# A hybrid attention and state-space layer: input squares, norms and decay sums placed by hand, and the output projection's first tiles loaded ahead

## The chip, the cores and the metric

The kernel runs on one NeuronCore of one Trainium2 chip. The metric is device time in microseconds (us) of a whole execution. Five engines run side by side: TensorE (PE, matmuls and transposes; PEld is its weight load), VectorE (DVE), ScalarE (ACT), GpSimd (POOL) and SyncE (SP), which here issues the DMAs. Each engine works through its own instruction list, so an instruction that waits holds back all that stands behind it there.

## The reference

The layer works on 2048 tokens of width 1024. The input is normalized, projected by one wide matrix `w_in`, and split among three groups of heads whose gated results are joined to 2048 columns, projected by `w_out`, added to the input and normalized again:

```python
hn = rms_norm(h, norm_in_w)
q, k, v, g_attn, z, xbc, dt_raw, q_mem, g_mem = split(hn @ w_in)
att = window_attention(rotary(q), rotary(k), v, sink) * silu(g_attn)      # 16 heads, 4 key heads, +-128 tokens
xs, bm, cm = split(silu(centred_depthwise_conv(xbc)))                     # 5 taps
y = ssd_scan(xs, dt[0], ...) + reversed(ssd_scan(reversed ...)) + d_skip * xs   # state-space scan, both directions
ssd = gated_group_rmsnorm(y, z, ssd_norm_w)
xat = softmax(q_mem @ mk.T) @ mv * silu(g_mem)                            # 4 heads onto 256 memory tokens
h = h + concat([att, ssd, xat]) @ w_out
return rms_norm(h, norm_out_w)
```

Inside a 128-token block the scan needs exp of differences of cumulative sums (the decay sums); from block to block a state is carried, once backward and once forward.

## The kernel before

**Tiling.** All is float32. Each product is three PE matmuls on high and low halves (`split3` L183); the halves come from an ACT cast to the high part (L195) and a DVE subtraction of the low one (L196). Nearly all PE matmuls carry the line of the helper `mm`, L177, so rows are told apart by their tiles. Weights of 128x1024 are loaded into `ws` (two buffers), or `xr` in the output projection, and split into `wh`, `wl` (three buffers each).

**Stages.** The main program walks four chunks of 512 tokens, from the last to the first (`for c` L920). A chunk computes keys, values and time steps, then four groups g of heads, each followed by two convolution pieces, the gate z and the memory heads' projections. After the chunks comes the output projection over sixteen blocks of 128 tokens (L957 on): `load_w` fetches the first weight tiles, `load_wo` the others, `early(c)` (L1004) does the attention and memory part of a block whose scan part is not ready, `out_block(c)` a whole block. `mixed` loads a block's joined results from DRAM (`mix_d`) into `mxl` and casts them to `mxh`.

**Side tasks.** Attention, memory attention, the scan's local part (`ssd_local`: load `xc` and the decay rows `fb`, decay sums L610 and L611, their exp L612, then the products), the carried states (`incoming`) and the joined forward result (`forward`) are generators. PE's order is written out by a planner: `mm` and `tr` advance a planner clock, and between two pieces of main work `tick` lets the side tasks take a step. `yield x` says that the task's next step is not due before x us of planner time; `limits` say how many tasks of a kind run at once, `need` runs tasks until one is done, `idle` lets planner time pass. ACT, DVE, POOL and SP are ordered by a list scheduler from priorities and readiness; it may place an instruction ahead of others that were written before it.

**Around the change.** The norm of the chunk after the present one is made in pieces: `rstd_cols` (called by `cols_x` at g = 1) loads 128x512 halves of x into `cu`, three buffers shared with the convolution, and takes squares with a row sum on ACT (L302), 28 in all; `norm_x` at the end of g = 2 loads the transposed input into `xp` and scales it on DVE (L349), 24 in all, storing it to `xn_d`. In `ssd_local` the next part's loads and decay sums are taken one step ahead of its products. In `forward`, y (L782) and z (L784) are loaded into `b0` and `b1`, POOL adds the carried part (L787) and multiplies by z (L789), ACT squares (L790), DVE adds the pairs (L792), and PE sums them.

Of the kernel before, what the change touches and what calls it, by code (L numbers as in the profile page):

```python
# [10 lines left out]
F32 = mybir.dt.float32  # L11
F32R = mybir.dt.float32r
# [24 lines left out]
def as32(ap):  # L37
    return ap.bitcast(F32)
# [7 lines left out]
def layer(ctx: ExitStack, tc: tile.TileContext, a: dict):  # L46
# [66 lines left out]
    clock = [0.0]  # L113
    queues = {"att": [], "mem": [], "ssd": [], "inc": [], "fwd": []}
    limits = {"att": 3, "mem": 1, "ssd": 1, "inc": 1, "fwd": 1}
    active = {k: [] for k in queues}
# [62 lines left out]
    def tr(out, in_):  # L179
        clock[0] += 0.11  # L180
        nc.tensor.transpose(out, in_, ident)  # L181

    def split3(out, pairs, start=True, stop=True):  # L183
# [109 lines left out]

    def rstd_cols(src, nblk):

        ss = misc.tile([P, 8], F32, name="ss", bufs=2)
        s2 = misc.tile([P, 2, 8], F32, name="s2")
        for b in range(nblk):
            for j in range(2):
# [6 lines left out]
        return ss  # L306

# [20 lines left out]
    def cols_x(c):  # L328
        s, _ = window(c)
        w = CH * (c + 1) - s  # L330
        return rstd_cols(a["x"][s:s + w, :], w // P)
# [10 lines left out]
    def norm_x(c, rb):  # L342
# [257 lines left out]
    def ssd_load(c, g):  # L600
        dt, fc, win = dts[c]
        xc = sp.tile([P, 4, P], F32, name="xc", bufs=2)
        nc.sync.dma_start(xc, xbc_d[4 * g:4 * g + 4, :, c * P:(c + 1) * P].rearrange("j p t -> p j t"))
        fb = sp.tile([P, 2, 4, P], F32, name="fb", bufs=1)
        nc.sync.dma_start(fb, f_d[c * 16:(c + 1) * 16].rearrange("(d h) t -> d h t", d=2)[:, 4 * g:4 * g + 4, :]
                          .partition_broadcast(P))
        ee = sp.tile([P, 4, P], F32, name="b0")
        for r in range(4):
            hd = slice(4 * g + r, 4 * g + r + 1)
            nc.scalar.activation(ee[:, r], fb[:, 0, r], AF.Identity, bias=fc[:, 0, hd])  # L610
            nc.vector.scalar_tensor_tensor(ee[:, r], fb[:, 1, r], fc[:, 1, hd], ee[:, r], ALU.add, ALU.min)  # L611
        nc.scalar.activation(ee, ee, AF.Exp)  # L612
        return xc, ee

    def ssd_local(blocks):
# [78 lines left out]
    def mem_attention(c, hd, qh, ql, gm, mkt, mvt):  # L694
# [48 lines left out]
    def incoming(c):  # L743
# [30 lines left out]
    def forward(c):  # L774

        if c == 0:
            while not ssd_t.done:
                yield 1.0
# [141 lines left out]
    for c in range(NPER - 1, -1, -1):  # L920
# [4 lines left out]
        for g in range(NG):  # L925
            if c and g == 1:
                cols = cols_x(c - 1)
            if c and g == 2:
                dg = diag_x(c - 1, cols)
            if g >= 2:  # L930
# [7 lines left out]
            if c and g == 2:  # L938
                norm_x(c - 1, rows_x(c - 1, dg))
            for i in range(2 * g, 2 * g + 2) if c else ((0, 1, 2, 3, 4), (5, 6, 7), (), ())[g]:  # L940
# [9 lines left out]
        if c == 0:  # L950
            fwd = [spawn("fwd", forward(b)) for b in range(NB)]
        if c:
            with tc.high_priority(offset=200):
                xs = prep_x(c - 1)
# [4 lines left out]
    for k in WO_K[:3]:  # L959
        woh[k], wol[k] = load_w(a["w_out"][k * P:(k + 1) * P, :])  # L960
    wx.close()
# [21 lines left out]
    def mixed(c, qs):  # L983

        mh, ml = {}, {}
        for q in qs:
            lo = fp.tile([P, 4, P], F32R, name="mxl", bufs=6)
            nc.sync.dma_start(as32(lo), mix_d[4 * q:4 * q + 4, :, c * P:(c + 1) * P].rearrange("j p t -> p j t"))  # L988
            hi = fp.tile([P, 4, P], F32R, name="mxh", bufs=5)
            split(hi, lo, as32(lo))  # L990
            for j in range(4):
                mh[4 * q + j], ml[4 * q + j] = hi[:, j], lo[:, j]
        return mh, ml

# [67 lines left out]
    rest_wo()  # L1062
    while last > 3 and not fwd[1].done:
        main(early(last))
        last -= 1
# [72 lines left out]
```

## Time and profile before

| what | value |
|---|---|
| time, median of three runs | 1852.75 us (1848.21 to 1855.27) |
| the profiled execution, its own time | 1848.8 us |
| its span, first to last instruction | 1847.1 us |
| mean granted TensorE clock | 0.985 of full |
| PE busy | 1755.7 us, 95% |
| DVE, ACT, POOL busy | 64%, 50%, 14% |
| DMA | 61% of sixteen engines, 188 GB/s |

PE is busy in 95% of the span, so its idle stretches are the first thing to look for, and behind each of them the instruction that ended it. A row of a timeline gives start and duration in us, engine, source line, operation, the tiles written and read, and in brackets the idle time before it with what ended that. The granted clock is the share of full speed, 0.5 or 1 at any moment.

### The profile page before, as it was taken

Reading aid. Unit: us, or ns where it says so; the run is one execution under the profiler, and the core shown is the slowest. Engines: PE = TensorE matmul, PEld = TensorE weight load, DVE = VectorE, ACT = ScalarE, POOL = GpSimd, SP = SyncE. Lnnn points to the kernel's source line nnn. Section 1 sums busy time; section 2 is a strip of 40 time slices with the busy share of each in tenths; the row PEclk is TensorE's granted clock in tenths of the full one; section 3 lists DMA queues with packets and bytes.
Section 4 is the critical chain, followed back from the end, with each engine's and each line's share of the span. In section 5 each row is a group of like instructions: output and inputs, shape, how many; then the busy total and the mean of one; then the engine's idle time right before and its main releaser. Section 6 shows DMA issues by size and latency. Waiting matters only on the chain. (4 is left out here: it accounts for less than half of the span.)

```text
span 1847.1 us, 26627 instructions
## 1 busy us (share of the span) xinstructions
PE 1755.7 (95%) x9242; PEld 1426.0 (77%) x9242; DVE 1179.9 (64%) x2681; ACT 921.4 (50%) x1985; POOL 260.3 (14%) x253
## 2 busy tenths in 40 slices
PE   7889999999799999999999989999998999999998
PEld 6878878877578787777778877778776777787886
DVE  7466666688576667778666777977677543443443
ACT  6237645664665566657555654656566411111121
POOL 1000000012200000121000002210111133333321
PEclk9989999999899999999999989999998999999999
DMA  7666364578653854776475466673658586566553
GB/s 237 211 197 187 123 214 146 152 241 244 210 169 122 268 165 150 240 245 206 142 211 161 133 205 195 190 214 118 197 179 265 165 251 182 164 180 180 171 176 120
DMA packets 264422, 347.59 MB, mean 188 GB/s; under 512 B 29536, under 2 KB 172000, under 8 KB 264288
## 3 DMA queue, kind: packets, MB, share of 16 engines
q1 hardware_dynamic: 264288, 345.90, 61.1%
q8 instruction: 73, 1.20, 0.3%
q14 instruction: 61, 0.50, 0.1%
HBM read 254.34 MB, written 91.49 MB: 187 GB/s over the span
## 5 line engine op out<-in xcount | busy, mean ns | idle before, releaser
L177 PE MATMUL pj<-xh,wh 128*128 128x512 f32 (+2 forms) x1296 | 506.6, 391 | 2.8 <-ACT xh L195 1.0
L177 PE MATMUL pj<-xl,wh 128*128 128x512 f32 (+2 forms) x1296 | 494.0, 381 | 4.8 <-DVE xl L196 4.8
L177 PE MATMUL pj<-xh,wl 128*128 128x512 f32 (+2 forms) x1296 | 494.7, 382 | 0.9 <-DVE wl L196 0.8
L196 DVE TENSOR_TENSOR wl<-ws,wh 128x1024 fp32r<-128x1024 f32 (+2 forms) x175 | 212.3, 1214 | 117.3 <-ACT wh L195 112.9
L177 PEld LDWEIGHTS pj<-xh,wl 128*128 128x128 f32 x1296 | 246.0, 190 | 46.9 <-DVE wl L196 2.7
L177 PEld LDWEIGHTS pj<-xh,wh 128*128 128x128 f32 x1296 | 246.7, 190 | 41.9 <-issue 3.7
L177 PEld LDWEIGHTS pj<-xl,wh 128*128 128x128 f32 x1296 | 246.8, 190 | 40.7 <-DVE xl L196 5.9
L195 ACT CAST wh<-ws 128x1024 fp32r<-128x1024 f32 (+2 forms) x175 | 180.0, 1029 | 179.3 <-PE pj L177 127.6
L546 DVE CUSTOM_DVE_ANT_0 pm<-s,band,sink 128x384 f32<-128x384 f32 (+1 forms) x256 | 150.3, 595 | 48.3 <-PE s L177 46.4
L554 ACT ACTIVATE pm<-pm,mx 128x385 f32<-128x385 f32 (+1 forms) x256 | 151.2, 595 | 55.5 <-DVE mx L552 55.5
L177 PE MATMUL pj<-woh,mxh 128*128 128x512 f32 x416 | 169.1, 407 | 0.0
L177 PE MATMUL pj<-woh,mxl 128*128 128x512 f32 x416 | 164.2, 395 | 0.0
L177 PE MATMUL pj<-wol,mxh 128*128 128x512 f32 x416 | 164.1, 394 | 0.0
L648 POOL TENSOR_TENSOR b<-nat,win 128x256 f32<-128x256 f32 x64 | 43.3, 697 | 841.2 <-ACT nat L632 841.2
L558 ACT ACTIVATE pm<-pm,den 128x384 f32<-128x384 f32 (+1 forms) x256 | 133.5, 595 | 6.9 <-DVE den L556 6.8
L572 ACT COPY pt<-t 128x512 f32<-128x512 f32 x120 | 69.4, 583 | 103.6 <-PE t L181 103.3
L195 ACT CAST mxh<-mxl 128x512 fp32r<-128x512 f32 x64 | 39.5, 617 | 162.8 <-DMA mxl<-mix_d 105.7
L181 PE MATMUL t<-ident,pm 128*128 128x128 f32 x736 | 103.8, 276 | 11.6 <-ACT nat L632 6.7
L181 PEld LDWEIGHTS t<-ident,pm 128*128 128x128 f32 x736 | 86.5, 142 | 34.6 <-ACT nat L632 7.6
L177 PE MATMUL s<-khh,qs 128*128 128x384 f32 (+1 forms) x256 | 94.7, 370 | 18.3 <-DVE mx L546 13.8
L484 DVE SCALAR_TENSOR_TENSOR cu<-raw,cw,cu 128x512 f32<-128x512 f32 (+2 forms) x128 | 99.3, 776 | 3.3 <-ACT cu L482 2.0
L177 PE MATMUL o<-pt,vg 128*64 128x256 f32 x736 | 93.8, 388 | 1.6 <-DVE dq L425 0.7
(222 smaller groups left out, 2842.8 us busy)
## 6 DMA issues: line engine op xcount, KB each, us to landing
ws<-in_w_in_dram SPq DMA_DIRECT2D x152, 512.0 KB, 4.2
q_d<-rt SPq DMA_DIRECT2D x32, 512.0 KB, 4.3
qs<-q_d SPq DMA_DIRECT2D x32, 512.0 KB, 6.1
fb<-f_d SPq DMA_DIRECT2D x32, 512.0 KB, 4.4
mxl<-mix_d SPq DMA_DIRECT2D x64, 256.0 KB, 4.1
mix_d<-ao SPq DMA_DIRECT2D x64, 128.0 KB, 3.5
xc<-xbc_d SPq DMA_DIRECT2D x32, 256.0 KB, 3.7
st_d<-carry SPq DMA_DIRECT2D x32, 256.0 KB, 3.9
```

The lines of the kernel that those rows point to most:

```text
L177: nc.tensor.matmul(out, lhsT=lhsT, rhs=rhs, start=start, stop=stop)
L181: nc.tensor.transpose(out, in_, ident)
L195: nc.scalar.copy(hi, x)
L196: (eng or nc.vector).tensor_tensor(lo, x, as32(hi), ALU.subtract)
L484: nc.vector.scalar_tensor_tensor(u, raw[:, r0 + k:r0 + k + cnt], cw[:, i, k:k + 1], u, ALU.mult, ALU.add)
L546: nc.vector.tensor_tensor_reduce(pm[:, r, :w], ss[:, :w], band[:, ms], 1.0, sink8[:, 4 * g + r:4 * g + r + 1], ALU.add, ALU.max, mx[:, r:r ...
L554: nc.scalar.activation(pm[:, r, :w + 1], pm[:, r, :w + 1], AF.Exp, bias=mx[:, r:r + 1], scale=0.125, accum_out=den[:, r:r + 1])
L558: nc.scalar.activation(pm[:, r, :w], pm[:, r, :w], AF.Copy, scale=den[:, r:r + 1])
L572: nc.scalar.copy(pts[j], tt)
L648: nc.gpsimd.tensor_tensor(xd[:, d], nat[:, 0:256].rearrange("p (r e) -> p r e", r=4), win[:, d, 4 * g:4 * g + 4].unsqueeze(2).broadcast_to ...
```

## The change

The squares and the scaling of the next chunk become side tasks of a new kind, "io", that load several tiles ahead and do one instruction per step; each such instruction is held by `pin` behind the instruction of its engine that was written just before it. The squares' task starts at g = 0 and uses `xp` (four buffers) in place of `cu`; the scaling task starts at g = 2. The decay sums move to the start of their own part, with the first of four head rows pinned. `forward` may run two blocks at once, with y in a buffer of its own kind. The output projection's first two joined tiles are loaded into the `ws` buffers before the `w_in` weights' pool is closed, and its later odd weight tiles no longer use `ws`.

```diff
-    limits = {"att": 3, "mem": 1, "ssd": 1, "inc": 1, "fwd": 1}
+    limits = {"att": 3, "mem": 1, "ssd": 1, "inc": 1, "fwd": 2, "io": 1}
+    pin = tc.keep_in_program_order
...
-    def rstd_cols(src, nblk):
+    def cols_x(c, out):
...
-                xn = misc.tile([P, XW], F32, name="cu", bufs=3)[:, :CH]
-                nc.sync.dma_start(xn, src[b * P:(b + 1) * P, j * CH:(j + 1) * CH])
-                nc.scalar.activation(xn, xn, AF.Square, accum_out=s2[:, j, b:b + 1])
+        for _ in range(3):
+            load()
+        yield 8.0
+        for i, (b, j) in enumerate(jobs):
+            pin(nc.scalar.activation(tiles[i], tiles[i], AF.Square, accum_out=s2[:, j, b:b + 1]))
+            load()
+            yield 3.0
...
         for kt in range(KT):
-            x32 = misc.tile([P, XW], F32, name="xp", bufs=4)[:, :w]
-            nc.sync.dma_start(x32, a["xT"][kt * P:(kt + 1) * P, s:s + w])
-            nc.vector.scalar_tensor_tensor(x32, x32, nw[:, kt:kt + 1], rb[:, :w], ALU.mult, ALU.mult)
-            nc.sync.dma_start(xn_d[kt, :, s:s + w], x32)
+            if kt == 4:
+                yield 6.0
+            pin(nc.vector.scalar_tensor_tensor(tiles[kt], tiles[kt], nw[:, kt:kt + 1], out["rows"][:, :w],
+                                               ALU.mult, ALU.mult))
+            nc.sync.dma_start(xn_d[kt, :, s:s + w], tiles[kt])
+            load()
+            yield 2.0
...
+    def ssd_decay(c, g, fb):
...
+            i1 = nc.scalar.activation(ee[:, r], fb[:, 0, r], AF.Identity, bias=fc[:, 0, hd])
+            i2 = nc.vector.scalar_tensor_tensor(ee[:, r], fb[:, 1, r], fc[:, 1, hd], ee[:, r], ALU.add, ALU.min)
+            if r == 0:
+                pin(i1)
+                pin(i2)
...
-            xc, ee = nxt
+            xc, fb = nxt
+            ee = ssd_decay(c, g, fb)
...
-        yield 3.0
+        yield 4.5
...
-        yield 7.0
+        yield 8.5
...
-        yy = sp.tile([P, 4, P], F32, name="b0")
+        yy = sp.tile([P, 4, P], F32, name="xc", bufs=2)
-        zz = sp.tile([P, 4, P], F32, name="b1")
+        zz = sp.tile([P, 4, P], F32, name=f"b{c % 2}")
...
-        yield 11.0
+        yield 13.0
...
+    first = [wsp.tile([P, D], F32R, name="ws", bufs=2).rearrange("p (u j t) -> p u j t", u=2, j=4) for _ in range(2)]
+    first = mixed_tiles(NB - 1, (0, 3), *([t[:, 0], t[:, 1]] for t in first))
     wx.close()
...
+    idle(clock[0] + 3.0)
...
-        ws = wsp.tile([P, D], F32, name="ws", bufs=2) if k % 2 else fp.tile([P, D], F32, name="xr", bufs=2)
+        ws = (wsp.tile([P, D], F32, name="ws", bufs=2) if k % 2 and pl is not wo else
+              fp.tile([P, D], F32, name="nwo") if k == 13 else fp.tile([P, D], F32, name="xr", bufs=2))
...
-        mh, ml = mixed(c, (0, 3))
+        mh, ml = mixed(c, (0, 3)) if begun else first
...
-    while last > 3 and not fwd[1].done:
+    while last > 3 and not fwd[2].done:
```

The first place is ACT's list in the last chunk, where the very first decay sums stand (`b_3434`, line L610, before; `b_3523`, line L642, after; `raw` and `cu` belong to the convolution, `xp` to the squares). Before:

```order
L195 CAST wh<-ws 128x1024
L469 COPY raw<-pj 128x320
L610 ACTIVATE b_3434<-fb,fc 128x128 x4
L482 ACTIVATE cu<-raw,cb,cw 128x638
L469 COPY raw<-pj 128x320
L612 ACTIVATE b_3434<-b_3434 128x512
```

After, in the same place of ACT's list, with the names as above and the squares at line L317:

```order
L483 ACTIVATE gm<-t 80x128
L317 ACTIVATE xp,s_862<-xp 128x512
L497 COPY raw<-pj 128x320
L317 ACTIVATE xp,s_862<-xp 128x512 x2
L198 CAST wh<-ws 128x1024
L497 COPY raw<-pj 128x320
L510 ACTIVATE cu<-raw,cb,cw 128x638
L642 ACTIVATE b_3523<-fb,fc 128x128 x3
L497 COPY raw<-pj 128x320
L317 ACTIVATE xp,s_862<-xp 128x512
L198 CAST wh<-ws 128x1024
```

Three of the four rows stand between the same copies of `raw` as the four did; the fourth, the pinned one, stands 136 rows further on, and three squares stand ahead of the three.

The second place is ACT's list where the output projection begins (`mxh<-mxl` and `ws<-ws` cast joined tiles, `woh` weight tiles, `pt` attention's transposed probabilities, `b_14023` and `b_14199` decay sums). Before:

```order
L670 COPY carry<-s 128x512
L632 COPY nat<-t 128x384
L195 CAST wh<-ws 128x1024
L227 ACTIVATE th<-pj 128x512
L572 COPY pt<-t 128x512
L195 CAST mxh<-mxl 128x512 x2
L610 ACTIVATE b_14023<-fb,fc 128x128 x4
L195 CAST mxh<-mxl 128x512
L612 ACTIVATE b_14023<-b_14023 128x512
L195 CAST mxh<-mxl 128x512 x2
L195 CAST woh_14066<-ws 128x1024
L195 CAST woh_14072<-xr 128x1024
```

After, on ACT from the copy of the carried state on:

```order
L706 COPY carry<-s 128x512
L642 ACTIVATE b_13933<-fb,fc 128x128
L668 COPY nat<-t 128x384
L647 ACTIVATE b_13933<-b_13933 128x512
L198 CAST wh<-ws 128x1024
L230 ACTIVATE th<-pj 128x512
L642 ACTIVATE b_14199<-fb,fc 128x128 x2
L600 COPY pt<-t 128x512
L642 ACTIVATE b_14199<-fb,fc 128x128
L198 CAST ws<-ws 128x512 x2
L198 CAST mxh<-mxl 128x512 x2
L582 ACTIVATE pm,den<-pm,mx 128x257 x4
```

Two decay sums now stand ahead of the copy of `pt`, and the first joined tiles' casts (`ws<-ws`) behind it; three more `mxh` casts and four more exps follow before the first `woh`.

The third place is POOL's list in the output projection, one block of `forward` (`state` and `carry` are the carried state, `fb` the carried part times its decay, `rn` the group norm, `b_16187` or `xc` holds y). Before:

```order
L787 TENSOR_TENSOR b_16187<-b_16187,fb 128x512
L789 TENSOR_TENSOR b_16187<-b_16187,b_16189 128x512
L595 TENSOR_TENSOR state<-state,dcy 128x512
L597 TENSOR_TENSOR state<-state,carry 128x512
L767 TENSOR_TENSOR fb<-fb 128x512
L801 TENSOR_TENSOR rn<-rn,neghalf 128x2
```

After, on POOL, the same six operations of a block at their new lines:

```order
L823 TENSOR_TENSOR xc<-xc,fb 128x512
L825 TENSOR_TENSOR xc<-xc,b_15871 128x512
L623 TENSOR_TENSOR state<-state,dcy 128x512
L625 TENSOR_TENSOR state<-state,carry 128x512
L803 TENSOR_TENSOR fb<-fb 128x512
```

The order is the same; y is in a buffer of its own. In PE's list the main matmuls (`pj`) between one block of `forward` and the next are 84 before (30, 42, 6 and 6 between its steps), and mostly 48 after (30, 6, 6 and 6).

## Rows read from the trace of the kernel before

**Rows 1.** Which engine is busy: page, part 1 (busy us, share, instructions)

```profile
PE 1755.7 (95%) x9242; PEld 1426.0 (77%) x9242; DVE 1179.9 (64%) x2681; ACT 921.4 (50%) x1985; POOL 260.3 (14%) x253
```

**Rows 2.** What PE waited for: line, releaser, us in total, times, longest

```profile
PE s L177 <- DVE mx L546: 14.7, 13, 6.8
...
PE t L177 <- DVE b L792: 8.1, 7, 2.0
...
PE t L177 <- DVE yo L804: 1.6, 3, 0.7
```

**Rows 3.** Stretches: us, busy PE, PEld, DVE, ACT, POOL, PEclk, DMA share, GB/s

```profile
123.80:134.00 10.20, 5.83 (x15) 4.83 (x16) 8.90 (x20) 5.28 (x10) 0.00 (x0) 0.50 0.36 101
400.00:435.00 35.00, 34.95 (x217) 28.39 (x216) 24.06 (x67) 15.46 (x34) 6.18 (x7) 1.00 0.95 290
468.60:503.00 34.40, 26.74 (x113) 20.92 (x114) 18.67 (x48) 26.32 (x65) 7.41 (x7) 0.85 0.65 199
1396.00:1408.00 12.00, 4.62 (x12) 3.46 (x12) 7.31 (x23) 5.07 (x11) 1.26 (x1) 0.57 0.99 332
```

**Rows 4.** Timeline of PE, 468 to 500 us

```profile
469.11 0.69 PE L177 MATMUL s<-khh,qs 128*128 128x384 f32 x1 [3.82 <-ACT carry L670]
...
492.64 0.33 PE L181 MATMUL t<-ident,pm 128*128 128x128 f32 x1 [1.12 <-ACT pm L558]
...
499.15 1.12 PE L181 MATMUL t<-ident,pm 128*128 128x128 f32 x4 [4.72 <-ACT nat L632]
```

**Rows 5.** Timeline of ACT, 467 to 499 us

```profile
467.87 0.63 ACT L302 ACTIVATE cu<-cu 128x512 f32<-128x512 f32 x1 [8.29 <-DMA cu<-in_x_dram]
...
498.01 0.63 ACT L302 ACTIVATE cu<-cu 128x512 f32<-128x512 f32 x1
...
498.63 0.47 ACT L632 COPY nat<-t 128x384 f32<-128x384 f32 x1
```

**Rows 6.** Timeline of PE and ACT around the first decay sums

```profile
128.17 0.69 PE L177 MATMUL s<-khh,qs 128*128 128x384 f32 x1 [6.76 <-DVE mx L546]
...
122.73 1.28 ACT L610 ACTIVATE b<-fb,fc 128x128 f32<-128x128 f32 x4 [6.24 <-DMA fb<-f_d]
```

**Rows 7.** DVE scaling the next tokens, and PE, around 962 us

```profile
962.37 0.75 DVE L349 SCALAR_TENSOR_TENSOR xp<-xp,nw,cu 128x512 f32<-128x512 f32 x1 [0.35 <-DMA xp<-in_xT_dram]
...
964.37 0.44 PE L177 MATMUL s<-khh,qs 128*128 128x384 f32 x1 [1.94 <-DVE mx L546]
```

**Rows 8.** Timeline of PE, memory attention, 1095 to 1098 us

```profile
1095.31 0.49 PE L177 MATMUL o<-pt,mvt 128*128 128x512 f32 x1 [2.06 <-ACT pt L727]
1097.68 0.80 PE L177 MATMUL o<-mpm,mvt 128*128 128x512 f32 x1 [1.88 <-DVE mpm L731]
```

**Rows 9.** Timeline of PE, start of the output projection

```profile
1403.38 0.79 PE L177 MATMUL pj<-wh,mxh 128*128 128x512 f32 x1 [8.86 <-ACT mxh L195]
```

**Rows 10.** Timelines of ACT and SP, 1398 to 1409 us

```profile
1402.71 1.30 ACT L195 CAST mxh<-mxl 128x512 fp32r<-128x512 f32 x2 [7.69 <-DMA mxl<-mix_d]
...
1408.57 1.04 ACT L195 CAST woh<-xr 128x1024 fp32r<-128x1024 f32 x1
...
1398.13 4.08 SPq L988 DMA_DIRECT2D mxl<-mix_d  x2
```

**Rows 11.** One block of forward: POOL and DVE timelines

```profile
1538.10 1.29 POOL L767 TENSOR_TENSOR fb<-fb 128x512 f32<-128x512 f32 x1 [2.46 <-DVE rn L800]
1539.35 1.15 POOL L801 TENSOR_TENSOR rn<-rn,neghalf 128x2 f32<-128x2 f32 x1
1550.89 1.29 POOL L787 TENSOR_TENSOR b<-b,fb 128x512 f32<-128x512 f32 x1 [10.39 <-DMA b<-y_d]
...
1536.73 1.29 DVE L764 TENSOR_TENSOR fb<-s,fb 128x512 f32<-128x512 f32 x2 [2.22 <-PE pj L177]
```

**Rows 12.** Its DMA issues: SP timeline, then page part 6

```profile
1552.21 1.26 SPq L756 DMA_DIRECT2D fb<-ef_d  x2
...
fb<-ef_d SPq DMA_DIRECT2D x32, 256.0 KB, 4.2
```

More of the change, by code (lines that the diff above doesn't have):

```diff
@@ L113, in layer @@
     clock = [0.0]
-    queues = {"att": [], "mem": [], "ssd": [], "inc": [], "fwd": []}
-    limits = {"att": 3, "mem": 1, "ssd": 1, "inc": 1, "fwd": 1}
+    queues = {"att": [], "mem": [], "ssd": [], "inc": [], "fwd": [], "io": []}
+    limits = {"att": 3, "mem": 1, "ssd": 1, "inc": 1, "fwd": 2, "io": 1}
     active = {k: [] for k in queues}
@@ L292, in small_constants, with load @@
         nc.vector.tensor_scalar(sink8, sink, 8.0, None, ALU.mult)
-    def rstd_cols(src, nblk):
+    def cols_x(c, out):
+        s, _ = window(c)
+        nblk = (CH * (c + 1) - s) // P
         ss = misc.tile([P, 8], F32, name="ss", bufs=2)
         s2 = misc.tile([P, 2, 8], F32, name="s2")
-        for b in range(nblk):
-            for j in range(2):
-                xn = misc.tile([P, XW], F32, name="cu", bufs=3)[:, :CH]
-                nc.sync.dma_start(xn, src[b * P:(b + 1) * P, j * CH:(j + 1) * CH])
-                nc.scalar.activation(xn, xn, AF.Square, accum_out=s2[:, j, b:b + 1])
+        jobs = [(b, j) for b in range(nblk) for j in range(2)]
+        tiles = []
+        def load():
+            if len(tiles) < len(jobs):
+                b, j = jobs[len(tiles)]
+                xn = misc.tile([P, XW], F32, name="xp", bufs=4)[:, :CH]
+                nc.sync.dma_start(xn, a["x"][s + b * P:s + (b + 1) * P, j * CH:(j + 1) * CH])
+                tiles.append(xn)
+        for _ in range(3):
[5 more added lines that the diff above has]
+            yield 3.0
         nc.vector.tensor_tensor(ss[:, :nblk], s2[:, 0, :nblk], s2[:, 1, :nblk], ALU.add)
@@ L305, in rstd_cols @@
         nc.gpsimd.tensor_tensor(ss[:, :nblk], ss[:, :nblk], neghalf[:, :nblk], ALU.pow)
-        return ss
+        out["cols"] = ss
     def diag(cols, n):
@@ L326, in window @@
         return s, e
[L328 to L331, printed above, removed]
     def diag_x(c, cols):
@@ L340, in rows_x, with norm_x, load @@
         return rb
-    def norm_x(c, rb):
+    def norm_x(c, out):
         s, _ = window(c)
         w = CH * (c + 1) - s
-        for kt in range(KT):
-            x32 = misc.tile([P, XW], F32, name="xp", bufs=4)[:, :w]
-            nc.sync.dma_start(x32, a["xT"][kt * P:(kt + 1) * P, s:s + w])
-            nc.vector.scalar_tensor_tensor(x32, x32, nw[:, kt:kt + 1], rb[:, :w], ALU.mult, ALU.mult)
-            nc.sync.dma_start(xn_d[kt, :, s:s + w], x32)
+        tiles = []
+        def load():
+            if len(tiles) < KT:
+                x32 = misc.tile([P, XW], F32, name="xp", bufs=4)[:, :w]
+                nc.sync.dma_start(x32, a["xT"][len(tiles) * P:(len(tiles) + 1) * P, s:s + w])
+                tiles.append(x32)
+        for _ in range(4):
+            load()
+        yield 8.0
+        while "rows" not in out:
+            yield 1.0
+        for kt in range(KT):
+            if kt == 4:
[3 more added lines that the diff above has]
+            nc.sync.dma_start(xn_d[kt, :, s:s + w], tiles[kt])
+            load()
+            yield 2.0
     def prep_x(c, rb=None, raw=None):
@@ L606, in ssd_load @@
                           .partition_broadcast(P))
+        return xc, fb
+    def ssd_decay(c, g, fb):
+        dt, fc, win = dts[c]
         ee = sp.tile([P, 4, P], F32, name="b0")
@@ L609, in ssd_load @@
             hd = slice(4 * g + r, 4 * g + r + 1)
-            nc.scalar.activation(ee[:, r], fb[:, 0, r], AF.Identity, bias=fc[:, 0, hd])
-            nc.vector.scalar_tensor_tensor(ee[:, r], fb[:, 1, r], fc[:, 1, hd], ee[:, r], ALU.add, ALU.min)
+            i1 = nc.scalar.activation(ee[:, r], fb[:, 0, r], AF.Identity, bias=fc[:, 0, hd])
[3 more added lines that the diff above has]
+                pin(i2)
         nc.scalar.activation(ee, ee, AF.Exp)
-        return xc, ee
+        return ee
     def ssd_local(blocks):
@@ L774, in forward @@
     def forward(c):
+        while not ssd_t.done:
+            yield 1.0
         if c == 0:
-            while not ssd_t.done:
-                yield 1.0
             spawn("inc", incoming(0))
         tl = slice(c * P, (c + 1) * P)
-        yy = sp.tile([P, 4, P], F32, name="b0")
+        yy = sp.tile([P, 4, P], F32, name="xc", bufs=2)
         nc.sync.dma_start(yy, y_d[:, :, tl].rearrange("j p t -> p j t"))
-        zz = sp.tile([P, 4, P], F32, name="b1")
+        zz = sp.tile([P, 4, P], F32, name=f"b{c % 2}")
         nc.sync.dma_start(zz, z_d[:, :, tl].rearrange("j p t -> p j t"))
@@ L925, in layer @@
         for g in range(NG):
-            if c and g == 1:
-                cols = cols_x(c - 1)
+            if c and g == 0:
+                ahead = {}
+                cols_t = spawn("io", cols_x(c - 1, ahead))
             if c and g == 2:
-                dg = diag_x(c - 1, cols)
+                need(cols_t)
+                dg = diag_x(c - 1, ahead["cols"])
+                norm_t = spawn("io", norm_x(c - 1, ahead))
             if g >= 2:
@@ L938, in layer @@
             if c and g == 2:
-                norm_x(c - 1, rows_x(c - 1, dg))
+                ahead["rows"] = rows_x(c - 1, dg)
             for i in range(2 * g, 2 * g + 2) if c else ((0, 1, 2, 3, 4), (5, 6, 7), (), ())[g]:
@@ L952, in layer @@
         if c:
+            need(norm_t)
             with tc.high_priority(offset=200):
@@ L960, in layer, with mixed_tiles @@
         woh[k], wol[k] = load_w(a["w_out"][k * P:(k + 1) * P, :])
+    def mixed_tiles(c, qs, los, his):
+        mh, ml = {}, {}
+        for q, lo, hi in zip(qs, los, his):
+            nc.sync.dma_start(as32(lo), mix_d[4 * q:4 * q + 4, :, c * P:(c + 1) * P].rearrange("j p t -> p j t"))
+            split(hi, lo, as32(lo))
+            for j in range(4):
+                mh[4 * q + j], ml[4 * q + j] = hi[:, j], lo[:, j]
+        return mh, ml
+    first = [wsp.tile([P, D], F32R, name="ws", bufs=2).rearrange("p (u j t) -> p u j t", u=2, j=4) for _ in range(2)]
+    first = mixed_tiles(NB - 1, (0, 3), *([t[:, 0], t[:, 1]] for t in first))
     wx.close()
@@ L983, in mixed @@
     def mixed(c, qs):
[L985 to L993, printed above, removed]
+        los, his = ([fp.tile([P, 4, P], F32R, name=nm, bufs=n) for _ in qs] for nm, n in (("mxl", 6), ("mxh", 5)))
+        return mixed_tiles(c, qs, los, his)
     def products(pf, mh, ml, order, first, last):
```

## The prediction

> **What bounds the kernel now.** I read the page's engine line first: PE is busy for 1755.7 of 1847.1 us [rows 1], so 91 us of PE's idle time, and what the half clock costs behind it, are all that a change of order can win. The chain that ended last says little more, since it is PE nearly throughout. Next I read the list of PE's waits by releaser, then PE's timeline for where each wait lies, and the timeline of the releasing engine for what held it. The reader is to see that the idle time is scattered, and that four places carry most of what this change can reach:
>
> - At 128 us PE waits 6.76 us for the maximum of the first scores; on ACT the first decay sums had waited 6.24 us for their rows of `fb` from DRAM, with the convolution behind them [rows 6].
> - At 469 to 499 us PE waits 3.82, two times 1.12, and 4.72 us [rows 4] (the second 1.12 stands at 494.10 us). ACT sat 8.29 us in front of a square whose half of x had not landed, with the copy of `carry` behind it; later a square stands directly ahead of the copy of `nat` [rows 5].
> - At 1403 us, where the output projection begins, PE waits 8.86 us for the first cast of a joined tile, which waited 7.69 us for its load; SP needed 4.08 us to issue two of these loads [rows 9, 10].
> - In `forward`, PE waits 8.1 us in seven pieces for the pair sums L792 and 1.6 us in three for L804: 9.7 us together [rows 2].
>
> After the long waits the clock is low: 0.50 of full, the 1.2 GHz level, over 123.8 to 134 us, and 0.85 and 0.57 as means of the other two stretches [rows 3]. At 0.50 the work done costs twice its time, so the 5.83 us busy in the first stretch hold 2.9 us of loss.
>
> I sum against the profiled execution, 1848.8 us. Plus is time won.
>
> **Squares of the next tokens.** The ten squares of chunk 1 leave the stretch 468 to 503 us. What can go is 3.82 + 2 x 1.12 + 4.72 = 10.8 us of idle time, and at most 15% of the 26.7 us busy there, 4.0 us, by the clock [rows 3, 4]: 14.8 us. All of the 3.82 is the square's. Of the 4.72, what ACT does before `nat` includes four squares after 488 us; at 0.63 us and a read of the sum each, they are some 3 us. I count 3.8 + 3 + 1 (of the 2.24) + 2.9 of clock = 10.7. Against that stand the 28 squares at their new places, 28 x 0.63 = 17.6 us of ACT's work, which ACT, busy 50% of the span [rows 1], mostly hides. A pinned one that is late holds ACT as 467.87 did, but three loads are ahead and a step of 3 us is long beside a 0.63 us square. I take +10, bounds -2 and +14.8.
>
> The order of ScalarE is first seen in the row: the copy of `carry` starts at 468.50 us right behind the square that had waited, though nothing else held it [rows 4, 5]. The Trainium skill, "TensorE: Matmul & The Clock Gate", section "Architectural detail: the array is 16× 32×32, not 1× 128×128", says that ScalarE and VectorE take their queue strictly in order. This speaks against the pins: by it every pinned square whose load is late costs what 467.87 us cost, while a scheduler that is left free could have put other work ahead. By this rule alone the term would be anything down to its low bound; by the loads being three ahead it is the +10.
>
> **Scaling of the next tokens.** DVE's waits for xT held scores' maxima behind them, as at 964 us, where PE waited 1.94 us after a scaling at 962.37 [rows 7]. PE's waits for these maxima, without the 6.8 us one, are 14.7 - 6.8 = 7.9 us in twelve pieces [rows 2]; 4.9 of them lie right behind scalings. With four loads ahead and steps of 2 us I take +3, bounds -2 and +5.
>
> **Decay sums.** The split takes them out of the step ahead, but only the first of four head rows is pinned. In the new order three rows of the first part's four still stand on ACT between the copies that the convolution needs, and wait for the same load. So the 6.76 us wait stays: 0, with +9.7 (6.76 + 2.9 of clock) if the three rows did not hold ACT, and -3 if the pinned rows later hold the copies of `nat` that now stand behind them.
>
> **Start of the output projection.** The most to win is 8.86 us and the clock's share: of the 12 us at a mean of 0.57, 4.62 us were busy, so at most 2 us [rows 3, 9]: +10.9. The two first tiles are loaded as soon as SP and the `ws` buffers allow, some 5 us before 1394.58, where the joined tiles' loads started. But three things are late next. First, ACT has two decay sums of the following part ahead of the copy of `pt`; their `fb` is loaded only after the tiles and three more DMAs on SP. With an issue at some 1393 us and the 4 us that such a load takes here, that copy comes at about 1399, and PE's four products with `pt` stand before the first `pj<-wh` of the projection: a wait of some 4 us. Second, their casts and subtractions follow, about 2 us. Third, the weights `woh` stand behind five `mxh` casts, which wait for their loads as the one at 1402.71 did, and behind four exps of attention. The DMA engines are 0.99 busy at 332 GB/s in this stretch [rows 3], so bringing two tiles forward does not bring all the others. Before, the second `woh` cast began at 1408.57 us, when nothing of PE waited for it [rows 10]. After, PE has 18 products for two tiles of weights, some 4 us, and then needs the next: if that cast stays near 1409 and its subtraction ends near 1411, PE waits 4 to 5 us there. With 4 + 2 + 4.5 of waits and 3 to 4 us for two falls of the clock the cost is 14 to 15 us, against 10.9 now. I take -4, bounds -10 and +10.9.
>
> **Forward.** y and z now load while the block before is still at work, which takes the front of each chain off PE's waits: up to 9.7 us [rows 2]. I take +7, since the L804 waits come behind the sums' own chain. What is late next is the chain from block to block. POOL's product with `fb` (1.29) frees that tile; SP issues two loads (1.26), they land after 4.2, DVE multiplies (1.29), POOL adds (1.29) and takes the power (1.15), and then the next product follows: 1.26 + 4.2 + 1.29 + 1.29 + 1.15 + 1.29 = 10.5 us [rows 11, 12]. Between two blocks PE has mostly 48 main products where it had 84; at the 0.23 us from one to the next that these take, with the block's own products, that is 14.5 us in place of 22. So 4 us of slack are left. Bounds -20 (below) and +9.7. The DMAs of this stretch are the same ones earlier, at 0.6 of the engines' time, so I give them no price.
>
> **The rest.** The longer pause before memory attention's last product aims at PE's waits of 2.06 and 1.88 us at 1095 us [rows 8], but PE's order there is unchanged, and ACT has two more instructions of the decay sums near its second cast: -0.5, at best +6.4 with the clock. The loads of x now come into stretches like 400 to 435 us, where the DMA engines are at 0.95 and 290 GB/s while PE is never idle [rows 3]: ten loads of 256 KB at 290 GB/s are 9 us of their time. If a third of that reaches PE through late weights, it is 3 us: -3, bounds -9 and 0. The other longer pauses move planner time alone.
>
> Row first: 0.95 of the engines' time at 290 GB/s and 0.99 at 332 [rows 3] show all loads on one set of sixteen engines. The Trainium skill, "DMA: Bandwidth & Descriptors", section "Issuing engines are not separate DMA queues", says that DMAs all end on the same sixteen engines and interleave there. That speaks against loading tiles ahead at the projection's start; by it the term is the -4, and if loads could pass each other freely it would be the +10.9.
>
> **The sum.** 10 + 3 + 0 - 4 + 7 - 0.5 - 3 = 12.5 us: 1836.3 us on the profiled execution. That one stands 3.95 us below the median of the three runs (1852.75), from which the same gain gives 1840.2. I take the middle, 1838.
>
> **The rivals.**
> - All waits go as meant, but for the first decay sums: 14.8 + 5 + 10.9 + 9.7 + 6.4 = 46.8 us, about 1804; with the first joined tile's gain and not the others, 1820. For it: the loads are ahead in every one. Against it: ACT's order at the projection, and PE's at 1095 us.
> - The gains are eaten by new small waits. If the pinned instructions and extra loads give back half of squares, scaling and forward, 12.5 becomes 2.5: about 1848, no change that can be measured. For it: the DMA engines' shares above, and 91 us of idle time that is made of small pieces. Against it: the 8.29 us wait of a square has one clear cause that is removed.
> - The chain from block to block in `forward` becomes the bound. Its place is the `ef_d` load and POOL; it decides from 14.5 us a block. Loads that land in 10 us in place of 4.2 make it 16.3, and over some 13 blocks 13 x 1.8 = 23 us are lost in place of 7 won: 1838 + 30 = 1868. For it: the queue of SP also holds the joined tiles' loads, one pair of which took 4.08 us to issue [rows 10]. Against it: POOL, where the chain runs, is 14% busy over the span.
> - The decay sums are not moved: that is in the forecast; if they were, 1828.
>
> **How the numbers follow.** Forecast, with its own range 1826 to 1846: 0.47. All or most as meant, 1804 to 1822: 0.13. Gains eaten, 1844 to 1858: 0.27. Slower, by the chain or by a dearer start of the projection, 1862 to 1870: 0.13. 0.5% is 9.3 us, about what can be told from no change here; faster than 1843.5 gets 0.47 + 0.13 = 0.60, within 0.27, slower than 1862 0.13. The range from 1812 to 1860 leaves about half of the second case and the last one out.
>
> **What the profile after would show.** Right: no wait of PE at 460 to 500 us over 2 us and a PEclk of 1.00 there; the wait of about 7 us behind the first decay sums still there; at the projection's start two or three waits of 3 to 5 us in place of one of 8.9; waits for L792's counterpart under 3 us in sum. Wrong: waits on squares or scalings at their new places; waits in `forward` that recur in every block and end with the carried part's DMA or with POOL; or a first part without the ACT wait for `fb`.

## The result, and the profile after

The changed kernel takes 1860.07 us, median of twenty runs, against 1851.25 us for the kernel before on the same chip: 1.0052 of it, interval 1.0036 to 1.0068. It is slower; the forecast was 1838 us, and faster. The profiled execution took 1862.17 us, with a span of 1860.5 us and a mean granted clock of 0.979.

The page of the kernel after, its first line of part 1 (answers [rows 1]) and the second of part 4, the shares of the chain that ended last:

```profile
PE 1765.7 (95%) x9242; PEld 1434.3 (77%) x9242; DVE 1200.7 (65%) x2681; ACT 921.7 (50%) x1985; POOL 256.2 (14%) x253
...
PE pj L177 46%; PE s L177 7%; PE o L177 5%; PE t L181 4%; DMA fb<-f_d 3%; ACT pm L582 3%; DVE wl L199 2%; DMA ws<-in_w_in_dram 1%; ACT pm L586 1%; DMA mxl<-mix_d 1%; ACT wh L198 1%; DVE pm L574 1%; DMA fb<-ef_d 1%; DVE cu L512 1%; DMA carry<-st_d 1%
```

PE is busy for 10 us longer with the same 9242 matmuls, and the chain passes through a load, `fb<-f_d`, for 3% of the span. On the page of before the chain could be followed back over the last 50 us alone (its PE share is 2%), so the two chains cannot be compared. What PE waited for, after (line, releaser, us in total, times, longest; answers [rows 2]):

```profile
PE s L177 <- DVE mx L574: 18.3, 12, 5.1
...
PE t L177 <- DVE yo L840: 8.8, 3, 5.1
...
PE s L177 <- DMA qs<-q_d: 4.0, 1, 4.0
```

The waits for L792's counterpart (L828) are gone, the waits for L804's counterpart (L840) went from 1.6 to 8.8 us, and the scores' maxima cost 18.3 in place of 14.7. PE's idle time in sum hardly changed: span less busy time is 91.4 us before and 94.8 after. The second stretch in the kernel before, columns as in [rows 3]:

```profile
447.00:460.00 13.00, 13.00 (x61) 10.90 (x60) 10.91 (x27) 7.00 (x13) 2.48 (x3) 1.00 0.80 222
```

The stretches of the kernel after:

```profile
127.00:137.40 10.40, 8.07 (x26) 6.75 (x27) 8.69 (x22) 3.38 (x6) 0.00 (x0) 0.67 0.41 117
447.00:460.00 13.00, 8.97 (x42) 7.23 (x41) 9.97 (x22) 6.28 (x14) 2.48 (x3) 0.97 1.01 251
468.60:503.00 34.40, 31.93 (x157) 24.01 (x155) 24.00 (x59) 21.17 (x48) 7.08 (x8) 0.95 0.44 146
1403.00:1434.00 31.00, 22.25 (x86) 15.83 (x86) 19.96 (x46) 21.33 (x46) 1.19 (x2) 0.78 0.77 244
```

From 468.6 to 503 us PE is busy 31.9 us in place of 26.7, at a PEclk of 0.95 in place of 0.85: the waits behind the squares are gone there. But 447 to 460 us, where PE had no idle time before, now has 4.0 us of it with the DMA engines at 1.01, and the 31 us from 1403 run at 0.78. Measured by work done, the gain is lost again: from the 1501st to the 2001st of PE's main products (`pj`), some 400 to 577 us, the kernel before takes 173.3 us and the changed one 176.1.

The new row that matters most is on ACT. The line of the decay sums before (durations, then what ACT's idle time in front of them waited for: us, times):

```profile
L610 ACT ACTIVATE b<-fb,fc x128: 384/390/443, 122.7 to 1429.6; 128x128 f32<-128x128 f32 x128
...
  POOL b L645: 33.1, 14
  DMA fb<-f_d: 6.2, 1
```

The same line after:

```profile
L642 ACT ACTIVATE b<-fb,fc x128: 384/394/436, 125.7 to 1451.5; 128x128 f32<-128x128 f32 x128
...
  DMA fb<-f_d: 55.1, 15
  POOL b L681: 21.2, 8
```

ACT waited 55.1 us for the rows `fb` in place of 6.2. How it comes about is seen in one part of the scan. ACT's timeline after:

```profile
449.90 0.40 ACT L642 ACTIVATE b<-fb,fc 128x128 f32<-128x128 f32 x1
450.20 0.47 ACT L668 COPY nat<-t 128x384 f32<-128x384 f32 x1
...
465.30 0.69 ACT L642 ACTIVATE b<-fb,fc 128x128 f32<-128x128 f32 x2 [9.26 <-DMA fb<-f_d]
```

DVE's timeline after, the same row's other half, then SP's:

```profile
450.33 0.35 DVE L643 SCALAR_TENSOR_TENSOR b<-fb,fc,b 128x128 f32<-128x128 f32 x1 [0.55 <-ACT b L642]
```

```profile
455.84 2.25 SPq L633 DMA_DIRECT2D fb<-f_d  x1
```

PE's timeline after, in the same place:

```profile
459.68 0.66 PE L177 MATMUL s<-khh,qs 128*128 128x384 f32 x1 [4.03 <-DMA qs<-q_d]
...
466.68 0.45 PE L177 MATMUL s<-khh,qs 128*128 128x384 f32 x1 [1.91 <-DVE mx L574]
...
472.72 0.49 PE L177 MATMUL s<-khh,qs 128*128 128x384 f32 x1 [1.79 <-DVE mx L574]
```

At 449.90 us stands the pinned sum of one part on ACT, and only when DVE's pinned row ends at 450.68 has the last reader left `fb`, which has a single buffer. SP has other DMAs to send first, the load of the next part's rows goes out at 455.84, and three free sums of that next part, which the scheduler put a few instructions behind the copy of `nat`, hold ACT for 9.26 us until it lands. This is the worst of the parts: its load took 9.4 us, the longest of the 32, whose median is 5.3 us. But the pattern is general. Before, the rows of each part but the first had landed 2.0 us or more ahead of their first sum (median 15.3 us); after, in 16 of these 31 parts the first sum starts within 0.1 us of the landing. Casts, copies and the convolution stand behind the sums, and PE waits 1.91 and 1.79 us for maxima. The 4.03 us at 459.68 are another matter: queries that come late while the next tokens' loads run.

### The profile page after: what moved, and what is told of

Read it like the earlier page. It is cut to its first block, busy times and chain, and to the rows that moved or that the text cites. A ratio compares the mean times of both kernels' runs of the same rounds, so it can differ in the third digit from the quotient of the medians.

```text
span 1860.5 us, 26606 instructions
## 1 busy us (share of the span) xinstructions
PE 1765.7 (95%) x9242; PEld 1434.3 (77%) x9242; DVE 1200.7 (65%) x2681; ACT 921.7 (50%) x1985; POOL 256.2 (14%) x253
## 4 chain that ended last, share of the span: by engine, by line
PE 63%; DMA 14%; DVE 9%; ACT 8%; issue 3%; POOL 2%; SPq 1%; DVEq 0%; POOLq 0%; ACTq 0%
PE pj L177 46%; PE s L177 7%; PE o L177 5%; PE t L181 4%; DMA fb<-f_d 3%; ACT pm L582 3%; DVE wl L199 2%; DMA ws<-in_w_in_dram 1%; ACT pm L586 1%; DMA mxl<-mix_d 1%; ACT wh L198 1%; DVE pm L574 1%; DMA fb<-ef_d 1%; DVE cu L512 1%; DMA carry<-st_d 1%
## 5 line engine op out<-in xcount | busy, mean ns | idle before, releaser
L199 DVE TENSOR_TENSOR wl<-ws,wh 128x1024 fp32r<-128x1024 f32 (+2 forms) x175 | 217.4, 1243 | 131.9 <-ACT wh L198 129.7
```

The costliest lines, as they stand in the source:

```text
L199: (eng or nc.vector).tensor_tensor(lo, x, as32(hi), ALU.subtract)
```

## The experiments

Ratios are to the kernel before on the same chip, and differences in us are taken from the ratios, since the medians come from different chips; 1% is 18.5 us. A difference of two rows is uncertain by some 4 to 6 us.

| run | what it is | ratio, interval | median us |
|---|---|---|---|
| - | the change | 1.0052, 1.0036 to 1.0068 | 1860.1 |
| e1 | change, sums one step ahead | 0.9948, 0.9927 to 0.9969 | 1841.3 |
| e2 | change, all four sums pinned | 1.0021, 1.0007 to 1.0036 | 1856.8 |
| e3 | change, projection's start as before | 1.0040, 1.0022 to 1.0057 | 1859.1 |
| e4 | change, forward as before | 1.0100, 1.0080 to 1.0120 | 1871.5 |
| e5 | change, no sum pinned | 0.9935, 0.9911 to 0.9959 | 1840.0 |
| e6 | change, two fb buffers | 0.9969, 0.9954 to 0.9984 | 1845.6 |
| e7 | tasks and split | 1.0000, 0.9982 to 1.0017 | 1851.0 |
| e8 | tasks alone | 0.9919, 0.9895 to 0.9943 | 1837.3 |
| e9 | change, memory's pause 3.0 | 1.0009, 0.9995 to 1.0024 | 1850.6 |
| e10 | tasks and forward | 0.9929, 0.9904 to 0.9955 | 1834.8 |
| e11 | tasks, forward, projection's start | 0.9928, 0.9915 to 0.9942 | 1835.2 |
| e12 | tasks and projection's start | 0.9948, 0.9930 to 0.9966 | 1839.2 |

"Tasks" are the squares and scalings as side tasks. Runs e1 to e4, e5 to e8 and e9 to e12 each shared a chip and the runs of the kernel before.

**e1, the sums one step ahead again.**

```diff
-        return xc, fb
+        return xc, ssd_decay(c, g, fb)
...
-            xc, fb = nxt
-            ee = ssd_decay(c, g, fb)
+            xc, ee = nxt
```

> The changed kernel, but the decay sums are taken one step ahead of their part, as before, with no pin. Theory A (the split is what costs: fb has one buffer, the next fb load can only start when the part's own pinned sum has read it, and the three free sums of the next part then hold ACT, which waited 55.1 us for fb in 15 pieces after, 6.2 us in one piece before): ACT's waits for fb fall below 12 us, the chunks win back about 10 us, time 1846 to 1851. Theory B (the start of the output projection and forward cost): 1855 to 1859, since only the 4 us wait for fb at the projection's start goes. Theory C (the loads of x that now fall into busy stretches cost): 1857 to 1861.

Measured 1841.3 us: 19 us come back from one edit, more than theory A expected, and the kernel that is left beats the one before. What ACT's idle time in front of the sums waited for, e1:

```profile
  DMA fb<-f_d: 1.5, 1
```

The load is no longer among the lines of the chain that the page lists, where the change has it with 3%. Theory C falls as the cause of the loss, since the loads of x stand in e1 where the change put them.

**e2, all four sums pinned.**

```diff
-            if r == 0:
-                pin(i1)
-                pin(i2)
+            pin(i1)
+            pin(i2)
```

> The changed kernel with all four decay sums of a part pinned where they are written, not the first alone. Theory A: the sums no longer run ahead of their load, ACT's waits for fb fall from 55 us to below 15 us, and the first part's wait of some 7 us at 128 us goes too: 1843 to 1852. Theory B: 1855 to 1859. Theory C: 1856 to 1861.

Measured 1856.8 us: this misses theory A's range and lies in those of B and C, which e3 and e1 rule out. ACT has no wait for `fb` left at all, and the chunks end earlier than before: the 4201st of PE's `pj` products, near their end, starts at 1302.8 us in place of 1311.1. The time is given back later. From the 4301st to the 4501st product e2 takes 103.4 us, the kernel before 91.6, and behind that some 5 us more. At the start of the output projection PE waits for the first weight tile, whose cast stands on ACT behind that of a joined tile which came late. PE's timeline of e2, then ACT's:

```profile
1405.08 0.79 PE L177 MATMUL pj<-woh,ws 128*128 128x512 f32 x1 [7.75 <-ACT woh L198]
```

```profile
1397.83 0.62 ACT L198 CAST mxh<-mxl 128x512 fp32r<-128x512 f32 x1 [6.78 <-DMA mxl<-mix_d]
```

PE's waits for copies of `nat` also rise, from 5.8 to 10.2 us; ahead of the longest, 4.07 us, the four pinned sums stand directly in front of the copy. The 55 us of ACT's waits were thus not the sum of the loss, and taking them away in this way only moved it.

**e3, the projection's start as before.** The two `first` lines and the `idle` are taken out, and `load_wo` and `early` are those of before.

> The changed kernel with the start of the output projection as before (no first tiles ahead, weights through ws again, no pause). Theory A: the chunks keep their loss; the projection's start has one wait of about 9 us in place of five of together 11.4 us with clock falls behind three of them: 1852 to 1857. Theory B (this start is the largest cost): 1848 to 1853. Theory C: 1857 to 1861.

Measured 1859.1: within the uncertainty of the change, and above the range of theory A too, which expected 3 to 8 us back from this start. Theory B, that this start is the largest cost, falls.

**e4, forward as before.** Limit 1, y in `b0`, z in `b1`, pauses 7 and 11, and the `early` blocks end with the second block of `forward` in place of the third.

> The changed kernel with forward as before (one block at a time, y in b0, the old pauses). PE waited in forward for 9.7 us in ten pieces before and for 8.8 us in three after, with clock falls behind two of the three. Theory B: forward costs some 3 us, 1855 to 1858. Theory A and C: within 2 us of the changed kernel, 1858 to 1862. My forecast's term of +7 would make this kernel slower than the changed one: 1866.

Measured 1871.5, outside all the ranges: undoing the new forward makes the changed kernel 9 us slower. My own term (1866) had the direction right, theory B had not.

**e5, no sum pinned.** The three lines with `pin` are taken out; the sums stay at the start of their part in the program's text.

> The changed kernel with the decay sums written at the start of their part as in the change, but none of the four pinned. Theory A in its sharper form (the one pinned sum keeps the single fb buffer until its own part, so the next load starts late, while the three free ones already stand on ACT behind the last copy of nat): all four now stand there together, fb comes free a part earlier, ACT's waits for the fb load fall from 55 us to below 10 us, and the time is that of the kernel with the sums one step ahead, 1838 to 1845. Rival D (what costs is that the sums are written later, pinned or not): ACT's waits for fb stay above 30 us and the time above 1853.

Measured 1840.0. The scheduler puts all four sums together behind the copy of `nat`, as before. What ACT's idle time in front of them waited for, e5:

```profile
  POOL b L678: 36.9, 16
  DMA fb<-f_d: 1.5, 1
```

So where the sums are written costs nothing; rival D falls. It is the one pinned among three free ones that costs.

**e6, two buffers for fb.**

```diff
-        fb = sp.tile([P, 2, 4, P], F32, name="fb", bufs=1)
+        fb = sp.tile([P, 2, 4, P], F32, name="fb", bufs=2)
...
-                xn = misc.tile([P, XW], F32, name="xp", bufs=4)[:, :CH]
+                xn = misc.tile([P, XW], F32, name="xp", bufs=3)[:, :CH]
```

The other places of `xp` and `fb` change alike, so that `forward`'s carried part has two buffers as well; a small tile of the time steps shares `gm`.

> The changed kernel, pins as they are, but fb has two buffers; to make room, xp has three buffers in place of four, and a small tile of the time steps lies in gm. Theory A: the load of the next part no longer waits for the pinned sum, ACT's waits for fb fall from 55 us to below 15 us and most of the 18 us between the changed kernel and the one with the sums ahead comes back: 1841 to 1850 (three xp buffers may cost some us). Rival D: 1855 or more, with the waits for fb still there.

Measured 1845.6, with the pins untouched. The same view for e6:

```profile
  POOL b L681: 38.8, 16
  DMA fb<-f_d: 1.2, 1
```

The 55 us go by the buffers, with the pins in place, and 15 of the 19 us with them, though `xp` has a buffer less. `forward`'s second buffer is not what won: from the 4501st `pj` product to the end the profiled executions of e6 and of the change both take 409.4 us. This shows the mechanism: the pinned sum keeps the only buffer, and the next load starts too late for the free sums.

**e7 and e8, the split with the tasks, and the tasks alone.** e8 is the kernel before with the two tasks and their pins; e7 adds the split with its one pin.

> The kernel before with the decay sums split and the first pinned, and with the squares and scalings as in the change; forward, the projection's start and the pauses are those of before. Theory A: the split costs some 18 us and the squares' and scalings' tasks win some 8: 1858 to 1866. Rival D says the same of this run. If the split cost only together with the new start of the projection, it would be 1842 to 1850.

> The kernel before with the squares' and scalings' tasks of the change and nothing else. By the recorded terms +10 and +3, less 3 for the loads in busy stretches: 1843. By the trace of the kernel with the sums ahead, whose last chunk ends 9.7 us earlier than before: 1842 to 1846. If pinned squares and scalings that wait for their loads (6.3 us at 119 us and 3.7 us at 620 us there) eat the gain: 1850 to 1856.

Measured 1851.0 and 1837.3. With the tasks on the base of before the split costs 0.8%, 15 us, and the tasks alone win 0.8%, 15 us. Both are outside their ranges: e8 was below its expected 1842 since the tasks won more, and e7, below 1858 for the same reason, came 1 us above the range in which the split costs only together with the new start. That it costs without this start is read from e7 beside e8. In e7 ACT waits for `fb` as in the change:

```profile
  DMA fb<-f_d: 58.5, 18
```

**e9, memory attention's pause as before.**

```diff
-        yield 4.5
+        yield 3.0
```

> The changed kernel with memory attention's pause at 3.0 as before, and nothing else undone. Theory E (the longer pause reorders PE so that a pinned scaling at about 620 us stands ahead of scores' maxima while its load is late: a wait of PE of 3 to 5 us and a clock fall, +8 us between 613 and 713 us in every kernel that has the 4.5, none in the two without it): no wait over 1.5 us there, 1850 to 1856 with the changed kernel at 1860. Rival (that wait is only an accident of the load's time, and the pause as such costs nothing, as recorded: -0.5): 1858 to 1862.

Measured 1850.6: the pause costs 0.4%, 8 us, as theory E expected. What it does is best seen in e1, which has the longer pause too; DVE's timeline, then PE's:

```profile
614.45 1.67 DVE L374 SCALAR_TENSOR_TENSOR xp<-xp,nw,cu 128x640 f32<-128x640 f32 x2
619.85 0.89 DVE L374 SCALAR_TENSOR_TENSOR xp<-xp,nw,cu 128x640 f32<-128x640 f32 x1 [3.73 <-DMA xp<-in_xT_dram]
```

```profile
621.72 0.69 PE L177 MATMUL s<-khh,qs 128*128 128x384 f32 x1 [4.69 <-DVE mx L574]
```

With the pause, memory attention's transposes and products fall in another place of PE's list, the planner lets three scalings come due close together, and the third, pinned, waits 3.73 us for its load with scores' maxima behind it. In the change a scaling at 630.03 us waits 2.17 us for its load, and PE 3.14 us behind it. In e8 and e9, with the old pause, no wait over 1.2 us is left between 527 and 790 us. All kernels agree on the place: from the 2001st to the 2251st `pj` product, some 577 to 668 us, the seven with the longer pause take 90.5 to 92.8 us, and the seven with the old one, the kernel before among them, 84.0 to 85.8. Between the profiled executions of the change and e9 this stretch makes 6.0 us (90.5 and 84.5); elsewhere they differ by up to some 6 us either way, which no run isolates.

**e10 to e12, the parts put together** without split and with the old pause.

> The squares' and scalings' tasks and the new forward; decay sums one step ahead, the projection's start and memory's pause as before. If the terms add up (tasks alone 0.992 of before; forward worth 9 us by the kernel with forward undone): 0.987, that is 1826 to 1833. If forward wins nothing without the new projection's start: 1835 to 1840.

> The same with the new start of the output projection. By the recorded term (-4) it is 4 us above the run without it: 1830 to 1837; beside the run with the sums ahead and the longer pause (0.9948) it shows the pause: 5 to 8 us less by theory E, the same by its rival.

> The squares' and scalings' tasks and the new projection's start, with forward and the pause as before and the sums one step ahead. By the recorded -4 for the start: 1839 to 1843 with tasks alone at 1837. If the start wins once no late decay sum stands ahead of the copy of pt (its wait for fb is gone): 1829 to 1835.

Measured 1834.8, 1835.2 and 1839.2. The first just misses both of its ranges, the second lies in its own, and the third is at the low end of the range with -4 for the start. The terms do not simply add up: beside tasks alone (0.9919), the new forward adds nothing that can be told (0.9929), and the new start costs between nothing (e11 beside e10) and 0.3% (e12 beside e8). In e10 forward's old waits have made place for others, such as this one of PE for a tile of the scan:

```profile
1534.60 1.62 PE L177 MATMUL s<-cbm,state 128*128 128x128 f32 x6 [3.05 <-DMA cbm<-xbc_d]
```

e11 beside e1 gives the pause once more, 0.2%, 4 us, with intervals that overlap. The best of these, e8, e10 and e11, beat the kernel before by 0.7 to 0.8% and the changed one by 1.2 to 1.3%, and are not told apart.

## Why the prediction was wrong, step by step

**Decay sums: the step that failed.** I took 0, with -3 as the low end. Measured are -19 us (change beside e1), -15 (e7 beside e8) and -15 (e9 beside e11). I saw that three of the four sums stay ahead, and asked only whether the first part's wait of 6.76 us goes. I did not ask, for the other 31 parts, when the load that they wait for can start. That is a question of the buffer: one `fb`, freed by the last of four rows, and this last row was the one that the change pinned to a later place. The low end covered copies of `nat` behind the pinned rows, not the free rows behind a late load. With -17 in place of 0 the sum turns from +12.5 to -4.5, and the forecast from faster to no change or slower.

**The first part's wait** did stay, but not as told: it is 5.07 us, and most of it is a pinned square's. ACT's timeline after, then PE's:

```profile
121.22 0.63 ACT L317 ACTIVATE xp<-xp 128x512 f32<-128x512 f32 x1 [6.67 <-DMA xp<-in_x_dram]
...
125.65 0.98 ACT L642 ACTIVATE b<-fb,fc 128x128 f32<-128x128 f32 x3 [1.49 <-DMA fb<-f_d]
```

```profile
129.33 0.69 PE L177 MATMUL s<-khh,qs 128*128 128x384 f32 x1 [5.07 <-DVE mx L574]
```

The square waited 6.67 us for its half of x, the sums behind it only 1.49. This is the price that the prediction named for a late pinned square, and a wait on a square at its new place was one of its signs of being wrong. The Trainium skill, "TensorE: Matmul & The Clock Gate", section "Architectural detail: the array is 16× 32×32, not 1× 128×128", has ScalarE take its queue strictly in order, and the trace agrees: the cast of `wh` and the copy of `raw` start only behind the square.

**Squares and scalings.** +10, +3 and -3 for their loads make +10; e8 measured +15, above the forecast and within the upper ends of 14.8 and 5. The -3 was too much on the tasks alone. That the loads collide with others is suggested by the wait of 4.03 us for `qs`, which stands in the change and not in e8, but no run isolates it. Nor does a run take the pins off the squares and scalings, so what these pins cost is not shown. The sign named for this gain, a PEclk of 1.00 from 460 to 500 us, is there in e8 and e1, and 0.92 in the change. The tasks' gain shows in the 1501st to 2001st `pj` product as well: 164.6 us in e8, 173.3 before, 176.1 in the change with its late sums.

**Memory attention's pause: mis-sized.** I took -0.5 since PE's order at the 1095 us stall is unchanged, which it is. But the pause reorders PE elsewhere, and it costs 8 us (change beside e9) or 4 (e1 beside e11). I had asked about the place that the edit aims at, and not about the other places that it moves.

**Start of the output projection.** Forecast -4, measured -2 (change beside e3), 0 and -5: right in size, within the uncertainty. The waits came where they were expected, four of 1.8 to 3.2 us where I had named two or three of 3 to 5. PE's timeline after:

```profile
1401.63 0.38 PE L177 MATMUL s<-khh,qs 128*128 128x256 f32 x1 [1.77 <-DVE mx L574]
...
1405.01 1.97 PE L177 MATMUL o<-pt,vg 128*64 128x256 f32 x8 [2.88 <-ACT pt L600]
...
1416.05 0.79 PE L177 MATMUL pj<-woh,ws 128*128 128x512 f32 x1 [3.08 <-ACT woh L198]
...
1428.11 0.66 PE L181 MATMUL t<-ident,pm 128*128 128x128 f32 x4 [3.20 <-ACT nat L668]
```

ACT's timeline after:

```profile
1403.79 0.69 ACT L642 ACTIVATE b<-fb,fc 128x128 f32<-128x128 f32 x2 [4.14 <-DMA fb<-f_d]
...
1408.48 0.62 ACT L198 CAST mxh<-mxl 128x512 fp32r<-128x512 f32 x1 [2.19 <-DMA mxl<-mix_d]
...
1414.97 1.98 ACT L198 CAST woh<-xr 128x1024 fp32r<-128x1024 f32 x2
```

The copy of `pt` stood behind the two sums and their late `fb` (4.14 us), the joined tiles' casts behind their loads, and the first two `woh` from 1414.97 on, where I had expected the second near 1409; some 5 us of this is that the chunks end later (the 4201st `pj` product at 1316.1 in place of 1311.1). In place of 8.86 us [rows 9] there are 10.9 in these four rows, and a PEclk of 0.78 over the stretch.

**Forward.** Forecast +7. Undone in the changed kernel it gives 9 us, in the other two pairs 4 us (e12 beside e11) and -2 (e8 beside e10), each with some 5 us of uncertainty. The wait moved along the chain as named. DVE's timeline after, then PE's:

```profile
1596.13 0.69 DVE L199 TENSOR_TENSOR mxl<-mxl,mxh 128x512 fp32r<-128x512 f32 x1 [7.31 <-ACT mxh L198]
1596.74 0.68 DVE L800 TENSOR_TENSOR fb<-s,fb 128x512 f32<-128x512 f32 x1
```

```profile
1601.09 1.19 PE L177 MATMUL t<-yo,ones 128*128 128x256 f32 x2 [5.09 <-DVE yo L840]
```

DVE's second product with `ef_d` (L800) came behind a subtraction of a joined tile, which had waited 7.31 us for its cast, and the group norm's `yo` was late by 5.09 us for PE. The chain from block to block was not the bound in every block: L840's waits are three. My count of 84 main products and 22 us a block before was too high, the trace has mostly 78 and 20.8 us (1606.3 to 1627.1); for after, 48 and 14.0 us (1569.3 to 1583.3) are near what I took, 48 and 14.5. By the profiled executions the new forward is worth less than 9 us: behind the 4301st `pj` product e4 takes 4.6 us longer than the change, and the other two pairs differ by 2.2 and -2.5 us.

**The rivals.** The measured 1860 lies between the ranges of two rivals, gains eaten (1844 to 1858) and slower (1862 to 1870), and neither gave the reason: what ate the gains is one mechanism and one reordering, and the slower case by forward's chain did not happen.

**The chain.** The prediction called the chain that ended last "PE nearly throughout". The page does not show that: its shares add up to some 2% of the span, the last 50 us. No term rests on it.

**The sum after the fact:** tasks +15, sums -15 to -19, pause -4 to -8, start 0 to -5, forward -2 to +9. Their middles give -7; measured is 0.52%, -9.6. Whether forward is really worth more in the changed kernel than beside the tasks alone stays open, since the pairs are uncertain by some 5 us each.

## What to carry to other kernels

When an edit splits a group of instructions that read one buffer and holds only one of them in place, ask when the last of them leaves the buffer, since the next load waits for that one while the free ones run ahead to wait for the load. A row in which an engine waits for a DMA once may be read together with the number of buffers behind it: pinning all, pinning none, or a second buffer each took away all or nearly all of the wait, though pinning all won back only 6 of the 19 us. And a change of a planner's pause is to be looked up in the whole order of the engine, not only at the stall for which it was made.

## What the runs showed of the hardware

The load of `fb` has a median of 4.4 us from issue to landing on the page of before and 5.3 on that of after; in the part shown above it took 9.4 us (issued at 455.84, the sum starts at 465.30), with the DMA engines at 1.01 in the stretch up to 460 us. Most of the lost time is not idle time: of the 13.4 us between the two spans, 3.4 are PE's idle time and 10.0 its longer busy time for the same matmuls. The mean granted clock fell from 0.985 to 0.979, which by the recorded clock is 54 us at the 1.2 GHz level before and 77 after; work done in these 23 us more takes up to 11 us longer, an estimate that covers the 10.
